# A Strassen pair whose sixth product has a PSUM bank of its own and whose seventh is issued behind the next pair's first, with PSUM tags by role and a later root and scan

## The chip, the cores and the metric

The kernel runs on one core of a Trainium2 chip. The metric is the device time of one execution in microseconds (us). The core's engines are TensorE (PE in the profile; PEld is its loading of stationary operands), VectorE (DVE), ScalarE (ACT), GpSimd (POOL) and SyncE (SP), which here only issues DMAs. Each engine works through its own queue of instructions in order. PE writes its sums to banks of PSUM, and DVE and ACT read them from there.

## The reference

The kernel computes one decoder block for one sequence of 2048 positions with a model width of 1024, in float32. Cut to what matters:

```python
h = rms_norm(x, g_norm) * (1 + scale) + shift        # shift, scale, gate from silu(c) @ w_mod
proj = h @ w_in                                       # 1024 -> 8 x 1024
x_rnn, z_rnn, q, k, v, z_attn, g_r, g_a = split(proj)
xc = causal_depthwise_conv(x_rnn)                     # width 4
r, i = sigmoid(xc @ w_a + b_a), sigmoid(xc @ w_x + b_x)   # 8 blocks of 128
a = exp(-8 * r * softplus(-lam)); bx = sqrt(1 - a * a) * i * xc
hr = scan(h_t = a_t * h_{t-1} + bx_t)                 # along the sequence
y_rnn  = (hr * silu(z_rnn)) @ w_out_rnn
o      = three dilated window attentions of rope(q), rope(k), v, merged
y_attn = (o * silu(z_attn)) @ w_out_attn
merged = sigmoid(g_r + b) * y_rnn + sigmoid(g_a + b) * y_attn
out = rms_norm(x + gate * (merged @ w_o), g_final)
```

## The kernel before

**Precision.** A float32 product is made of three matmuls: each operand is split into a high and a low part, and `mm3` (L150) sums high by high, high by low and low by high in one PSUM bank (the matmuls are recorded in `mm`, L148). An operand's high part is made by ACT (L202, L156), the low part by POOL (L162) or DVE (L165).

**The projection by Strassen pairs.** Every part of the projection but v is computed by Strassen and Winograd's scheme of seven products instead of eight. One pair covers two blocks of 128 output columns by two chunks of 512 positions (`CH`), that is one half of the sequence. There are 28 pairs, and the outer loop (L933 and on) goes through all of them twice, for the first half of the sequence (f = 0) and for the second (f = 1). A product sums four blocks of 128 along the contraction, so it is 4 x 3 = 12 matmuls of 128 x 512. The left operands are sums of blocks of the weights: for f = 0 they are formed as they are needed (`left_operands`, L250: the sums on DVE at L256, L257, L259 and L264, the split on ACT and POOL) in a ring of seven tiles S, and stored to DRAM (`sD`, from ACT's queue); for f = 1 they are loaded again from `sD` by SP's queue (`load_next`), each load following the product that frees a tile. The right operands, B11 to B22 and T1 to T4, are made once for each half.

`strassen` (L314) records the products of a pair in this order, with four PSUM tiles of the pool `pj`, which has five banks that rotate under one tag:

| product | right operand | bank | what reads the bank |
|---|---|---|---|
| 1 | B11 | X | ACT copies it to u1 (L340) |
| 2 | T2 | Z | DVE: u2 = Z + u1 (L341) |
| 3 | T3 | W | DVE: u3 = W + u2 (L346) |
| 4 | T1 | V | DVE: V + u3 is output block (1, 1), "ev4" |
| 5 | B21 | X, on top | ACT: X is output block (0, 0) |
| 6 | T4 | W, on top | DVE: W + u2 is block (1, 0), "ev6" |
| 7 | B22 | V, on top | DVE: V + u2 is block (0, 1), "ev7" |

The three evictions on DVE are `total` (L387); their destination is named ev, zs, xr or t after the kind of pair. Products 5, 6 and 7 accumulate onto what is in the bank, so 6 cannot start before u3 has read W, and 7 not before ev4 has read V. The pairs follow one another without a break, and a new tile takes the bank that was allocated five tiles earlier.

**The recurrence.** In each half eight of the pairs, one for each block m of the recurrence, hold x_rnn in their row 0 and z_rnn in row 1 (`recurrent`). Each is followed by one or two pairs for gates or for the part of q and k that isn't rotated ("plain"); 22 pairs make up this stage. After them come two pairs with rotated columns (`rotated_pairs`) and four plain ones. The steps of the recurrence are recorded at fixed distances, counted in products, behind product 5 of the pair for the first chunk and 7 products later for the second (`steps_after`, L775 and on): tap 0 (ACT makes xc, L714), taps 1 (three multiply-adds on DVE, L720), split 2, gates 4 (6 matmuls each into the pool `pg` of three banks), sigmoids 5 (L733), decay 6 (POOL L737, DVE L738), exponentials 7 (ACT Tanh, Exp, Square, L743 to L745), root 8 (DVE L749, ACT Sqrt L750), scan 9 (DVE: t times gi at L754, the scan at L755), finish 10 (DVE: times the gate zs, L760), then halves and store. zs has two buffers, xc one.

**What sets the order.** The attention and output part has an order written out by hand. In the projection the kernel records operations in program order, and a scheduler at build time lays out each engine's queue from its own estimate of durations; evictions, u1, u2 and u3 are recorded with high priority. At run time an instruction of a queue waits in place until what it needs is done, and all that stands behind it waits too.

## Time and profile before

| | us |
|---|---|
| three runs | 2355.1, 2352.55, 2354.84 |
| median | 2354.84 |
| the profiled execution | 2357.67 |
| its span, first to last instruction | 2355.9 |
| PE busy | 2232.7 |
| DVE busy | 1322.5 |
| ACT busy | 1187.2 |
| POOL busy | 953.0 |

The mean granted clock of TensorE is 0.983 of full speed. By stages, in us from the span's start: opening and values of f = 0 to about 210 (the first pairs start at 152); recurrence, gate and plain pairs of f = 0 from 210 to 640; rotated and last plain pairs to 752; values of f = 1 to 873; recurrence, gate and plain pairs of f = 1 to 1350; rotated and last plain pairs to 1448; attention, outputs and the final norm to the end.

A row of the timeline gives the start (us), the duration (us), engine, line, operation, output<-inputs by the program's names, shapes and the number of instructions joined in the row; in square brackets stands how long the engine idled before it, and what ended that. A row of the waits gives the engine, what it worked on, what it waited for, and then the total in us, the number of times and the longest. Matmuls are pipelined, so the end of one overlaps the start of the next.

### The profile page before, as it was taken

The page shows a single profiled execution, that of the slowest core. Times are in us where ns is not written, and L with a number is a line of the kernel's source. Part 1 is how long each engine was busy: PE and PEld are TensorE (multiplying, and loading weights), DVE is VectorE, ACT ScalarE, POOL GpSimd, SP SyncE. Part 2 cuts the span into 40 slices and gives each one's busy share as a digit, 9 for nine tenths or more (in the row PEclk, how much of TensorE's full clock was granted, in tenths as well). Part 3 has the DMA queues.
Part 4 walks back from the last instruction along what each step waited for, and adds up shares of the span by engine and source line. Part 5 has one row for each costly group of instructions (what it writes and reads, how often), then busy time and mean ns, then how long its engine had stood idle before and what let it go on. Part 6 is the DMA issues. An engine that isn't in the chain of part 4 may idle for free.

```text
span 2355.9 us, 33999 instructions
## 1 busy us (share of the span) xinstructions
PE 2232.7 (95%) x11397; PEld 1878.1 (80%) x11397; DVE 1322.5 (56%) x2430; ACT 1187.2 (50%) x2358; POOL 953.0 (40%) x732
## 2 busy tenths in 40 slices
PE   6999999999989999999999998989999898989998
PEld 6997777777777897778888876878888797968887
DVE  6837666757586625344544461456666778645343
ACT  4636656666642635555544411565667787622111
POOL 1356656665556534333211120354455656422000
PEclk9999999999999999999999999999999999999999
DMA  7376877677779669999777778888898888799732
GB/s 257 102 226 221 275 262 262 235 267 249 244 251 282 189 200 323 322 308 326 239 235 233 247 226 267 263 251 278 266 293 274 242 242 249 223 336 304 252 122 97
DMA packets 420946, 585.44 MB, mean 249 GB/s; under 512 B 72518, under 2 KB 278562, under 8 KB 419748
## 3 DMA queue, kind: packets, MB, share of 16 engines
q1 hardware_dynamic: 382932, 463.53, 63.4%
q10 hardware_dynamic: 37648, 119.70, 13.4%
q8 instruction: 90, 1.47, 0.3%
q14 instruction: 84, 0.69, 0.1%
q0 software_dynamic: 192, 0.05, 0.0%
HBM read 367.14 MB, written 216.01 MB: 248 GB/s over the span
## 4 chain that ended last, share of the span: by engine, by line
PE 59%; DMA 12%; DVE 8%; ACT 5%; issue 4%; POOL 2%; SPq 1%; ACTq 1%; DVEq 0%; POOLq 0%
PE pj L148 41%; PE pq L148 7%; PE o L148 4%; PE sc L148 4%; DMA R<-in_w_in_dram 2%; PE pg L148 1%; PE pT L1163 1%; POOL S L162 1%; DMA vraw<-vN 1%; PE pT L1176 1%; ACT L744 1%; DMA S<-sD 1%; DMA gw<-in_w_mod_dram 1%; DMA meT<-fg 1%; DMA wD<-s 1%
## 5 line engine op out<-in xcount | busy, mean ns | idle before, releaser
L148 PE MATMUL pj<-T,S 128*128 128x512 f32 x4704 | 1119.6, 397 | 30.0 <-DVE ev L387 17.9
L148 PEld LDWEIGHTS pj<-T,S 128*128 128x128 f32 x4704 | 887.6, 189 | 249.8 <-DVE ev L387 24.5
L148 PE MATMUL pj<-yh,S 128*128 128x512 f32 x1024 | 374.5, 409 | 17.7 <-ACT yh L156 10.3
L162 POOL TENSOR_TENSOR S<-R,S 128x512 fp32r<-128x512 f32 x168 | 245.7, 1474 | 272.4 <-ACT S L202 99.6
L148 PEld LDWEIGHTS pj<-yh,S 128*128 128x128 f32 x1024 | 197.0, 192 | 55.6 <-ACT yh L156 11.1
L148 PE MATMUL pj<-yl,S 128*128 128x512 f32 x512 | 204.9, 401 | 1.6 <-POOL yl L162 0.6
L1079 ACT ACTIVATE pp<-pp,st 128x256 f32<-128x256 f32 (+3 forms) x256 | 133.9, 524 | 114.2 <-DVE st L1078 113.4
L148 PE MATMUL pj<-S,T 128*128 128x256 f32 x1152 | 158.4, 292 | 4.6 <-ACT S L156 1.4
L148 PEld LDWEIGHTS pj<-S,T 128*128 128x128 f32 x1152 | 147.8, 196 | 6.2 <-POOL S L162 1.8
L162 POOL TENSOR_TENSOR S<-s,S 128x512 fp32r<-128x512 f32 x84 | 113.9, 1358 | 73.4 <-ACT S L202 39.0
L165 DVE TENSOR_TENSOR ptl<-pT,pth 128x384 fp32r<-128x384 f32 (+1 forms) x160 | 97.8, 628 | 67.1 <-ACT pth L156 64.9
L1078 DVE CUSTOM_DVE_ANT_0 pp<-sc,msk 128x256 f32<-128x256 f32 (+3 forms) x256 | 105.0, 449 | 32.3 <-PE sc L148 29.5
L720 DVE SCALAR_TENSOR_TENSOR xc<-xr,par,xc 128x512 f32<-128x512 f32 x96 | 84.1, 876 | 68.6 <-ACT xc L714 67.9
L1143 ACT ACTIVATE pp<-pp,M 128x256 f32<-128x256 f32 (+3 forms) x256 | 118.0, 523 | 9.0 <-DVE M L1267 9.0
L148 PEld LDWEIGHTS pj<-yl,S 128*128 128x128 f32 x512 | 98.8, 193 | 18.8 <-DMA yl<-yaT 2.7
L162 POOL TENSOR_TENSOR kq<-kraw,kq 128x512 fp32r<-128x512 f32 (+1 forms) x64 | 100.1, 1574 | 31.8 <-ACT kq L156 31.6
L341 DVE TENSOR_TENSOR u<-pj,u 128x512 f32<-128x512 f32 x56 | 38.4, 686 | 131.4 <-PE pj L148 81.6
L162 POOL TENSOR_TENSOR vh<-vraw,vh 128x256 fp32r<-128x256 f32 (+1 forms) x64 | 66.6, 1041 | 111.8 <-ACT vh L156 94.3
L162 POOL TENSOR_TENSOR wh<-vraw,wh 128x640 fp32r<-128x640 f32 (+1 forms) x32 | 48.4, 1511 | 129.1 <-ACT wh L156 60.5
L148 PE MATMUL pq<-ol,mh 128*128 128x512 f32 x256 | 100.5, 393 | 0.0
L148 PE MATMUL pq<-oh,mh 128*128 128x512 f32 x256 | 97.9, 393 | 2.1 <-ACT mh L156 2.1
L148 PE MATMUL pq<-oh,ml 128*128 128x512 f32 x256 | 99.5, 389 | 0.0
(297 smaller groups left out, 3848.0 us busy)
## 6 DMA issues: line engine op xcount, KB each, us to landing
sD<-S ACTq DMA_DIRECT2D x196, 512.0 KB, 3.9
S<-sD SPq DMA_DIRECT2D x196, 512.0 KB, 5.4
S<-wD SPq DMA_DIRECT2D x128, 512.0 KB, 5.6
R<-in_w_in_dram SPq DMA_DIRECT2D x136, 256.0 KB, 4.2
wD<-s ACTq DMA_DIRECT2D x64, 256.0 KB, 5.4
T<-in_w_mod_dram SPq DMA_DIRECT2D x8, 1024.0 KB, 11.6
vN<-ev SPq DMA_DIRECT2D x64, 128.0 KB, 2.1
zaT<-ev SPq DMA_DIRECT2D x32, 256.0 KB, 4.7
```

The source lines that it names most:

```text
L148: last_mm[0] = nc.tensor.matmul(o, lhsT=l, rhs=r, start=st, stop=sp, **kw).ins
L162: nc.gpsimd.tensor_tensor(o, i, h.bitcast(F32), ALU.subtract)
L165: return nc.vector.tensor_tensor(o, i, h.bitcast(F32), ALU.subtract).ins
L341: nc.vector.tensor_tensor(u2[:], Z[:], u1[:], ALU.add)
L720: nc.vector.scalar_tensor_tensor(xc, xr[:, i : i + CH], cw(i), xc, ALU.mult, ALU.add)
L744: nc.scalar.activation(a, y, AF.Exp, scale=-1.0)
L1078: nc.vector.tensor_tensor_reduce(pdst, s_ps, mask, 1.0, 3e38, ALU.add, ALU.min, m_)
L1079: nc.scalar.activation(pdst, pdst, AF.Exp, bias=m_, scale=-1.0, accum_out=l_)
L1143: nc.scalar.activation(pp, pp, AF.Copy, scale=w)
L1163: nc.tensor.transpose(pt[:, c0 + j * P : c0 + (j + 1) * P], pp[i][:, k * P : (k + 1) * P], ident)
L1176: nc.tensor.transpose(pt[:, c * P : (c + 1) * P], pp[:, half * P : (half + 1) * P], ident)
```

## The change

Five things are changed.

- Product 6 has a PSUM tile of its own, Y, of the tag "Z"; it no longer accumulates onto W, and output block (1, 0) is Y + u3 instead of W + u2. The bank W is finished with product 3.
- Product 7 isn't recorded at the end of its pair. It is kept in `behind` with its left operand already taken, and recorded by `last_product` after product 1 of the next pair (or at the end of a stage).
- The PSUM tiles of the pairs have tags by role: X with two banks, Z, W and V with one each, five in all as before. The value stage goes through them in the order X, Z, W, X, V (`pj_tile`).
- Root, scan and finish are recorded at 9, 11 and 12 products behind product 5 instead of 8, 9 and 10; halves and store follow at 12, for f = 1 at 13 and 14. zs has three buffers instead of two, and xc two instead of one.
- The loads of f = 1 follow the set of operands used, in order, since product 7's operand is now used after a later one. The tables of closures bind their loop variables, `finish_late` runs a step's list itself, and six of the seven `next_even` steps come one product later.

```diff
--- before.py
+++ after.py
@@ -213,7 +213,8 @@
 
     def finish_late():
         while late:
-            run_late(min(late))
+            for fn in late.pop(min(late)):
+                fn()
 
     def steps_after(start, steps):
         for lag, fn in steps:
@@ -279,7 +280,7 @@
 
 
 
-    loaded, n_loaded = [], [0]
+    loaded, n_loaded, used = [], [0], set()
 
     def load_next():
         n = n_loaded[0]
@@ -287,7 +288,7 @@
         if n < 28 * 7:
             t = s_tile([P, 2, KH, P])
             nc.sync.dma_start(t[:].bitcast(F32), sD[n])
-            loaded.append(t)
+            loaded.append((n, t))
         else:
             k = n - 28 * 7
             if k < 3:
@@ -319,40 +320,66 @@
             for _ in range(NS):
                 load_next()
 
-        def prod(ps, b, first, last):
-            s = loaded.pop(0) if f else next(ops)
+        def take():
+            return (f, *loaded.pop(0)) if f else (f, 7 * x, next(ops))
+
+        def prod(ps, b, first, last, op=None):
+            f, i, s = op or take()
             bh, bl = B[b]
             for k in range(KH):
                 mm3(ps[:], s[:, 0, k, :], s[:, 1, k, :], bh[:, k, :], bl[:, k, :],
                     first=first and k == 0, last=last and k == KH - 1, skip_group_check=True)
             n_prod[0] += 1
             if f:
-                load_next()
+                used.add(i)
+                while n_loaded[0] - NS in used:
+                    load_next()
             run_late(n_prod[0])
 
-        X = T(pj, [P, CH], F32, "pj")
+        X = T(pj, [P, CH], F32, "X", bufs=2)
         prod(X, "B11", True, False)
-        Z = T(pj, [P, CH], F32, "pj")
+        last_product()
+        Z = T(pj, [P, CH], F32, "Z")
         prod(Z, "T2", True, True)
         u1 = T(up, [P, CH], F32, "u1", bufs=1)
         u2 = T(up, [P, CH], F32, "u2", bufs=2)
         with tc.high_priority():
             nc.scalar.activation(u1[:], X[:], AF.Copy)
             nc.vector.tensor_tensor(u2[:], Z[:], u1[:], ALU.add)
-        W = T(pj, [P, CH], F32, "pj")
-        prod(W, "T3", True, False)
+        W = T(pj, [P, CH], F32, "W")
+        prod(W, "T3", True, True)
         u3 = T(up, [P, CH], F32, "u3", bufs=1)
         with tc.high_priority():
             nc.vector.tensor_tensor(u3[:], W[:], u2[:], ALU.add)
-        V = T(pj, [P, CH], F32, "pj")
+        V = T(pj, [P, CH], F32, "V")
         prod(V, "T1", True, False)
         done(1, 1, V, u3)
         prod(X, "B21", False, True)
         done(0, 0, X, None)
-        prod(W, "T4", False, True)
-        done(1, 0, W, u2)
-        prod(V, "B22", False, True)
-        done(0, 1, V, u2)
+        Y = T(pj, [P, CH], F32, "Z")
+        prod(Y, "T4", True, True)
+        done(1, 0, Y, u3)
+        op = take()
+
+        def last():
+            prod(V, "B22", False, True, op)
+            done(0, 1, V, u2)
+        behind.append(last)
+
+
+    behind = []
+
+    def last_product():
+        while behind:
+            behind.pop()()
+
+
+    pj_tags, n_pj = ("X", "Z", "W", "X", "V"), [0]
+
+    def pj_tile(shape):
+        tag = pj_tags[n_pj[0] % 5]
+        n_pj[0] += 1
+        return T(pj, shape, F32, tag, bufs=1 + (tag == "X"))
 
     def output_weights():
 
@@ -423,7 +450,7 @@
     pR = pools.open("pR", side="right", bufs=1)
     wS = pools.open("wS", side="right", bufs=1)
     wq = pools.open("wq", side="right", bufs=1)
-    pj = pools.open("pj", bufs=5, space=PSUM)
+    pj = pools.open("pj", bufs=1, space=PSUM)
     pg = pools.open("pg", bufs=3, space=PSUM)
     vx = pools.open("vx", bufs=1)
 
@@ -609,7 +636,7 @@
     def values_by_halves(ev, m, ws, n):
 
         names = ("B12", "B22") if n % 2 else ("B11", "B21")
-        pss = [T(pj, [P, 2, 256], F32, "pj") for g in range(2)]
+        pss = [pj_tile([P, 2, 256]) for g in range(2)]
         for kh in range(2):
             (hh, hl), (wh, wl) = B[names[kh]], ws[kh]
             for g in range(2):
@@ -634,7 +661,7 @@
 
         names = ("B12", "B22") if n % 2 else ("B11", "B21")
         for g in range(2):
-            ps = T(pj, [P, 2, 256], F32, "pj")
+            ps = pj_tile([P, 2, 256])
             for r in range(2):
                 js = slice((2 * g + r) * P, (2 * g + r + 1) * P)
                 for k in range(KT):
@@ -687,7 +714,7 @@
         start = [0]
 
         def z_part(j, ps, u):
-            z = zs[j] = T(rp, [P, CH], F32, "zs", bufs=2)
+            z = zs[j] = T(rp, [P, CH], F32, "zs", bufs=3)
             total(z[:], ps, u)
             sg = []
 
@@ -711,7 +738,7 @@
             def tap():
                 nc.scalar.activation(xr[:, 0:3], xtail[:, m, :], AF.Copy)
                 nc.scalar.activation(xtail[:, m, :], xr[:, CH : CH + 3], AF.Copy)
-                nc.scalar.activation(new("xc"), xr[:, 0:CH], AF.Identity, scale=cw(0),
+                nc.scalar.activation(new("xc", bufs=2), xr[:, 0:CH], AF.Identity, scale=cw(0),
                                      bias=par[:, C_CB + m : C_CB + m + 1])
 
             def taps():
@@ -774,7 +801,7 @@
                 start[0] = n_prod[0]
             steps_after(start[0] + 7 * j, (
                 (0, tap), (1, taps), (2, split), (4, gates), (5, sigmoids), (6, decay), (7, exponentials),
-                (8, root), (9, scan), (10, finish), (11 if f else 10, halves), (12 if f else 10, store)))
+                (9, root), (11, scan), (12, finish), (12 + f, halves), (12 + 2 * f, store)))
 
         def done(i, j, ps, u):
             (z_part if i else x_part)(j, ps, u)
@@ -842,7 +869,7 @@
     def rotated_pairs(qp, f, Ct, St):
 
         for base, dstT, qs in QK:
-            def rotated(i, j, ps, u):
+            def rotated(i, j, ps, u, dstT=dstT, qs=qs):
                 n = 2 * f + j
                 cq = slice(j * CH, (j + 1) * CH)
                 t0 = T(qp, [P, CH], F32, "t0", bufs=NT0[f])
@@ -873,7 +900,7 @@
             cuts.append(pieces)
         for base, dstT, qs in QK:
             for t in range(0, 6, 2):
-                def plain(i, j, ps, u):
+                def plain(i, j, ps, u, t=t, dstT=dstT, qs=qs):
                     n = 2 * f + j
                     t0 = plain_at[0]()
                     scaled(t0, ps, u, qs)
@@ -888,7 +915,7 @@
     def gate_pairs(ep, f):
         for m in range(0, KT, 2):
             for base, dst, b0 in ((5 * D, zaT, None), (6 * D, grT, C_BG), (7 * D, gaT, C_BG + 8)):
-                def gate(i, j, ps, u):
+                def gate(i, j, ps, u, m=m, dst=dst, b0=b0):
                     n = 2 * f + j
                     t = T(ep, [P, CH], F32, "ev", bufs=3)
                     v = ps
@@ -952,6 +979,7 @@
             for _ in range(1 + (m % 4 > 0)):
                 next(plain if n % 6 == 3 else gates)
                 n += 1
+        last_product()
         finish_late()
         pools.close("rp")
         qp = pools.open("qp", bufs=1)
@@ -971,7 +999,8 @@
             if n == 5 and f == 0:
 
                 for p in range(7):
-                    late.setdefault(n_prod[0] + p + 1, []).append(lambda p=p: next_even(p))
+                    late.setdefault(n_prod[0] + p + 1 + (p > 0), []).append(lambda p=p: next_even(p))
+        last_product()
         finish_late()
         for n in sorted(after_prod):
             run_late(n)
```

## The prediction, made before the changed kernel was run

> **What bounds the kernel now.** I read the head of the page first, then busy time by stage, then TensorE's waits, then the rows of single pairs.
>
> ```profile
> span 2355.9 us, 33999 instructions
> PE 2232.7 (95%) x11397; PEld 1878.1 (80%) x11397; DVE 1322.5 (56%) x2430; ACT 1187.2 (50%) x2358; POOL 953.0 (40%) x732
> ```
>
> TensorE (PE) is busy in 95% of the span; no other engine passes 56%. The change removes no matmul, so it can only win idle time of PE. The next view gives the busy time by stage (first column the window, second its length, then PE, PEld, DVE, ACT, POOL, the granted clock):
>
> ```profile
> 210.00:640.00 430.00, 407.27 (x1716) 322.78 (x1715) 276.55 (x301) 264.27 (x434) 258.25 (x184) 0.99 0.74 252
> 640.00:752.00 112.00, 103.94 (x451) 82.74 (x450) 80.68 (x136) 40.02 (x72) 59.68 (x41) 0.98 0.81 257
> 873.00:1350.00 477.00, 469.82 (x2012) 378.06 (x2011) 207.39 (x266) 243.92 (x383) 132.20 (x101) 1.00 0.85 280
> 1448.00:2356.00 908.00, 857.72 (x4770) 739.03 (x4768) 517.72 (x1301) 460.58 (x1163) 341.96 (x288) 0.97 0.79 245
> 1100.00:1200.00 100.00, 100.00 (x431) 80.63 (x430) 48.42 (x60) 54.85 (x88) 23.86 (x19) 1.00 0.77 251
> ```
>
> The recurrence and gate pairs run in 210 to 640 (first half of the sequence, f = 0) and 873 to 1350 (f = 1): PE idles 430.00 − 407.27 = 22.7 us in the first, 7.2 in the second. Attention and outputs (1448 to the end) are untouched by the edit, and in the two programs' orders by engine they are the same; I cost them at nothing. The last row gives the yardstick: 100.00 us held 431 matmuls without a gap, 0.232 us each, so a product of 12 takes 2.78 us, and two take 5.57. Who ends PE's idle time (total us, times, longest):
>
> ```profile
> PE pj L148 <- DVE ev L387: 17.9, 14, 3.3
> PE pj L148 <- DVE zs L387: 3.1, 2, 1.8
> PE pj L148 <- DVE u L346: 3.0, 2, 1.7
> PE pj L148 <- DMA S<-sD: 2.1, 1, 2.1
> ```
>
> The first three are the change's target. Their places, for two pairs of f = 0 (6, from 286 us, and 7), the longest (980.75), and one with a long tail (550.91):
>
> ```profile
> 298.81 5.96 PE L148 MATMUL pj<-T,S 128*128 128x512 f32 x25
> 305.41 8.20 PE L148 MATMUL pj<-T,S 128*128 128x512 f32 x34 [0.65 <-DVE ev L387]
> ...
> 325.11 3.05 PE L148 MATMUL pj<-T,S 128*128 128x512 f32 x12 [1.71 <-DVE u L346]
> 330.49 6.79 PE L148 MATMUL pj<-T,S 128*128 128x512 f32 x28 [2.33 <-DVE ev L387]
> ...
> 550.91 5.30 PE L148 MATMUL pj<-T,S 128*128 128x512 f32 x15 [2.22 <-DVE ev L387]
> ...
> 980.75 4.61 PE L148 MATMUL pj<-T,S 128*128 128x512 f32 x12 [3.31 <-DVE ev L387]
> ```
>
> 325.11 is product 6 of pair 7, which accumulates onto product 3's bank and waits until u3 (L346) has read it. 305.41, 330.49, 550.91 and 980.75 start product 7, which accumulates onto product 4's bank and waits for that product's eviction, ev4 (L387 on DVE). Why ev4 is late shows DVE's own queue:
>
> ```profile
> 302.92 1.23 DVE L720 SCALAR_TENSOR_TENSOR xc<-xr,par,xc 128x512 f32<-128x512 f32 x1 [3.26 <-ACT xc L714]
> ...
> 305.28 1.16 DVE L720 SCALAR_TENSOR_TENSOR xc<-xr,par,xc 128x512 f32<-128x512 f32 x1
> ...
> 307.57 1.80 DVE L720 SCALAR_TENSOR_TENSOR xc<-xr,par,xc 128x512 f32<-128x512 f32 x1
> 309.29 1.27 DVE L755 TENSOR_TENSOR_SCAN y<-a,htail,t 128x512 f32<-128x512 f32 x1
> 310.48 1.72 DVE L259 TENSOR_TENSOR R<-R,R 128x512 f32<-128x512 f32 x1
> 312.12 2.09 DVE L760 TENSOR_TENSOR zs<-y,zs 128x512 f32<-128x512 f32 x1
> 314.14 1.27 DVE L387 TENSOR_TENSOR ev<-pj,u 128x512 f32<-128x512 f32 x2
> ...
> 326.61 0.69 DVE L749 SCALAR_TENSOR_TENSOR t<-y,t 128x512 f32<-128x512 f32 x1 [1.55 <-ACT y L745]
> 329.14 0.69 DVE L754 TENSOR_TENSOR t<-t,gi 128x512 f32<-128x512 f32 x1 [1.84 <-ACT t L750]
> 329.75 0.68 DVE L387 TENSOR_TENSOR ev<-pj,u 128x512 f32<-128x512 f32 x1
> ...
> 335.46 0.69 DVE L259 TENSOR_TENSOR R<-R,R 128x512 f32<-128x512 f32 x1
> ...
> 336.66 0.69 DVE L387 TENSOR_TENSOR ev<-pj,u 128x512 f32<-128x512 f32 x1
> ```
>
> In pair 7, ev4 (329.75) stands behind L754 (t·gi), which waits 1.84 us for ACT's square root, and behind the root's L749, which waits 1.55. In pair 6 a convolution tap (L720) waits 3.26 us for ACT's xc in front of it.
>
> **The change part by part.**
>
> *What goes.* Product 6 gets a bank of its own, so the 3.0 us for u3 go. Product 7 comes a product (2.78) later, root and scan one and two products later, and in the changed program's order on DVE ev4 now stands ahead of t·gi: of the 17.9 + 3.1 us only what exceeds 2.78 could stay (3.31 − 2.78 = 0.5, and ev4 is earlier too). I take all: 24.0 us. Two of these waits have a tail at half clock: the 12 matmuls of 980.75 took 4.61 us where those of 325.11 took 3.05, and the 15 of 550.91 took 5.30 against 15 × 0.232 + 0.17 = 3.65; 1.6 each, 3.2 together. Together 27.2 us; the lower bound is nothing, if every wait reappears elsewhere. By the Trainium skill ("TensorE: Matmul & The Clock Gate", table of clock states) the half rate comes after an idle window of about 3.4 us; here 2.22 us of idle time were followed by it and 2.33 (330.49, 28 matmuls in 6.79) were not, so the trace departs from the page; by the rule neither tail would be due to its wait, and the sum would be 3.2 less.
>
> *What comes: product 2 of the next pair.* Product 6 of a pair and product 2 of the next now share the one bank "Z", so the next pair's second product must wait for ev6, product 6's eviction. Between lie the next product 1 and the late product 7: ev6 has 5.57 us from product 6's end. How late is it by the trace of before? Pair 6: the run from 298.81 holds the last 11 matmuls of product 5, the 12 of product 6, and 2 of the next product 1, so product 6 ended at 298.81 + 23 × 0.232 = 304.15; ev6 is the first of the two at 314.14 and ended at 314.82. That is 10.67, 5.1 over. Pair 7: product 6 (325.11) ended at 327.99, ev6 (336.66) at 337.35: 9.36, 3.8 over. The first and the last of the late pairs:
>
> ```profile
> 185.71 12.47 PE L148 MATMUL pj<-T,S 128*128 128x512 f32 x53
> 198.30 0.68 DVE L387 TENSOR_TENSOR ev<-pj,u 128x512 f32<-128x512 f32 x1
> ...
> 607.79 6.44 PE L148 MATMUL pj<-T,S 128*128 128x512 f32 x27
> 621.46 0.68 DVE L387 TENSOR_TENSOR ev<-pj,u 128x512 f32<-128x512 f32 x1
> ```
>
> Pair 1 (product 6 ends 18 matmuls into that run, 189.9; 9.1, 3.5 over) and pair 20 (25 matmuls in, 613.6; 8.5, 3.0 over). Of pairs 1 to 20, fifteen are over, by 46.5 us together. That is the upper end for f = 0. Two things shorten it. In the changed order the three taps of the second xc no longer stand between ev4 and ev6 but ahead of u2, five products earlier: without the time they take there (pair 6: 3.97 us of the rows 302.92, 305.28 and 307.57; 2.5 to 2.9 in the other such pairs) 20.8 us are left. And the waits of L749 and L754 (3.4 us in pair 7), inside the same stretch in seven pairs, shrink with the later root and scan, whose inputs from ACT are then a product or two old; those seven (2, 4, 7, 10, 13, 15, 18: 11.9 of the 20.8) then come to about nothing. What stays are pairs 1, 3, 6, 9, 12, 17 and 20: 0.8, 0.9, 1.1, 1.6, 1.7, 2.7, 0.1: 8.9 us. For f = 1, DVE is emptier (207 us busy in 477), and only pair 30 is far over, by 8.6, of which 3.5 are this:
>
> ```profile
> 946.00 0.69 DVE L387 TENSOR_TENSOR zs<-pj,u 128x512 f32<-128x512 f32 x1 [3.49 <-DMA yaT<-zs]
> ```
>
> With three zs buffers that wait goes, taps take 2.3; I keep 2.9. New waits: 11.8 us, bounds 0 and 46.5. I take a value near the low end because the instructions that make the lateness are seen to move.
>
> The Trainium skill speaks against me here ("SBUF — State Buffer", Who interferes with whom): a VectorE instruction with two SBUF inputs and a GpSimd one that reads SBUF block each other for a whole instruction. The rows agree: L259 takes 1.72 us at 310.48 and 0.69 at 335.46. Were one more such meeting to fall ahead of ev6 in each of the seven pairs, 7 × 1.03 = 7.2 us would be added.
>
> *Next product 4 behind ev7.* One bank "V": the next product 4 waits for product 7's eviction, which has two products again, products 2 and 3. ev7 follows ev6 directly (314.14, x2), and product 7 is itself a product later; I take 0, bounds 0 and 2.8 (one product).
>
> *Later root and scan, one xc buffer more.* The same instructions, later. The last recurrent pair of each half runs out over more products, all covered by PE's. The changed program has one table load more:
>
> ```profile
> L750 ACT ACT_TABLE_LOAD x32 | 41.1, 1283 | 1.6 <-DMA S<-sD 1.0
> ```
>
> 1.28 us on ACT, busy 264 of 430: 0, at most 1.3.
>
> *Product 7's operand held longer.* One of seven S tiles comes free a product later, in f = 1 also its reload on SP's queue. The only wait for a reload is the 2.1 us above; 0, bounds −2.1 and +2.8.
>
> *Rotated pairs, 640 to 752.* Evictions there wait for the rotary tables:
>
> ```profile
> 687.65 0.69 DVE L387 TENSOR_TENSOR t<-pj,u 128x512 f32<-128x512 f32 x1
> ```
>
> This is ev7 of pair 22, 25 us after its product. In the changed order pair 23's product 4 must follow it; the order puts three other products (pair 24's 1, 3 and 5) ahead of it. Counting products to the start of that product 4, 15 precede in both. I take 0, ±3. In the opening the value tiles rotate through the banks by role: ±2.
>
> Sum: −24.0 − 3.2 + 11.8 = −15.4 us. The profiled execution took 2357.67 (span 2355.9), 2.8 over the median 2354.84; against the first 2342.3, against the second 2339.4. **Predicted: 2339 us.**
>
> **The rivals.**
>
> *A. Everything goes.* No new wait: 2354.8 − 27.2 = 2328. For it: the changed order and the emptier f = 1 half. Against it: ev6 still follows scan, finish, s1 and R on DVE, 4 to 7 us of work.
>
> *B. The gap moves.* The waits of L749 and L754 stay although recorded later, because ACT is equally late; then new waits are 20.8 + 2.9 = 23.7 and the time is 2354.8 − 27.2 + 23.7 = 2351. For it: the planner had already put the next product 1 ahead of product 7 in places (the 2 matmuls at the end of 298.81's run), so this edit is partly there.
>
> *C. The Z bank binds (slower).* One mechanism: product 2 of the next pair waits for ev6, with DVE's queue as long as before because the taps, moved ahead of u2, still push everything behind them back by their 3.26 us wait for ACT. The lateness is then the 46.5 us, and the time 2354.8 − 27.2 + 46.5 = 2374. It decides from 27.2 / 15 = 1.8 us per late pair on, that is from ev6 7.4 us after product 6. Against it: five products lie between u2 and ev6, and DVE is idle 36% of that stage.
>
> **How the numbers follow.** My forecast (2332 to 2346) has 0.45, A 0.17, B 0.18, C 0.20. What a measurement can tell from no change is 0.2%, 4.7 us: faster is under 2350.1, slower over 2359.5. Faster: 0.45 + 0.17 + a third of B = 0.68; same: the rest of B, 0.12; slower: C, 0.20. The range reaches below to A with 3 us of the rotated pairs (2325) and above into the milder half of C (2361), which leaves about 0.05 and 0.13 out.
>
> **What would show it.** Right: the waits of PE for ev at product 7 and for u at product 6 gone, new ones at product 2 of the next pair of 5 to 20 us together, all in f = 0 and at most 2.7 each, PE idle under 14 us in the stage that is now 210 to 640; no zs wait for a DMA on DVE; the attention stage still 908 us. Wrong: waits at product 2 or 4 of over 27 us; an L720 or L754 that waits for ACT still in front of ev4 or ev6; half-clock windows after new gaps of over 2.2 us; or a rotated stage longer than 115 us.

## The result

The changed kernel takes 2359.8 us (median) beside 2354.26 us for the kernel before: 1.0023 times as long, 95% interval 1.0012 to 1.0034. Forecast were 2339 us and a range that ended at 2361 with the chances on faster; it went the other way, by 5.5 us.

The profiled execution of the changed kernel took 2354.95 us (span 2353.2), at the low end of its runs. Its page still says that TensorE is busy in 95% of the span. The stages tell more, bounded here and below by the first matmul of pairs 0, 22, 28 and 50 in each trace (columns as before: window, length, PE, PEld, DVE, ACT, POOL, granted clock, DMA share, GB/s). First the kernel before, pairs 0 to 21 of f = 0 and of f = 1:

```profile
152.27:640.63 488.36, 462.77 (x1946) 367.19 (x1945) 320.14 (x343) 297.94 (x491) 298.28 (x211) 0.99 0.75 254
...
873.82:1336.45 462.63, 455.45 (x1946) 366.34 (x1945) 203.33 (x255) 242.59 (x381) 132.20 (x101) 1.00 0.85 279
```

Then the changed kernel, the same pairs:

```profile
146.21:645.75 499.54, 466.48 (x1947) 372.81 (x1945) 342.74 (x345) 299.88 (x493) 301.26 (x213) 0.97 0.72 250
...
880.14:1334.86 454.72, 453.59 (x1947) 365.21 (x1945) 205.28 (x255) 244.15 (x381) 131.57 (x101) 1.00 0.85 285
```

The f = 1 pairs gained 7.9 us, and hold almost no idle time (454.72 − 453.59 = 1.1 us). The f = 0 pairs lost 11.2 us, with VectorE 22.6 us longer busy, and TensorE's clock granted at 0.97 instead of 0.99. The rest of the span in these two executions: opening 152.3 to 146.2, rotated pairs and values 233.2 to 234.4, rotated pairs of f = 1 126.8 to 123.0, attention and outputs 892.6 to 895.3. Over all the traces of this study the opening lies between 144.7 and 152.3 us and the attention part between 887.6 and 898.0, also among kernels whose orders there are the same, so these two are scatter and hide 5.5 us easily in one execution; the medians of the runs decide. What TensorE waits for in the changed kernel:

```profile
PE Z L148 <- DVE ev L414: 32.4, 11, 6.2
...
PE X L148 <- ACT t L863: 4.8, 1, 4.8
...
PE Z L148 <- DVE t L414: 3.8, 2, 2.3
```

The waits of products 6 and 7 of the kernel before (24.0 us) are gone, every one. In their place stands product 2 of the next pair, which waits for ev6 on the shared bank Z: 32.4 us, all but 0.3 of it in the f = 0 pairs. Two of these on TensorE, at pair 10 (waiting for ev6 of pair 9) and at pair 15 (for ev6 of pair 14):

```profile
368.87 2.96 PE L148 MATMUL X<-T,S 128*128 128x512 f32 x12
371.66 2.95 PE L148 MATMUL V<-T,S 128*128 128x512 f32 x12
376.31 1.87 PE L148 MATMUL Z<-T,S 128*128 128x512 f32 x7 [1.70 <-DVE ev L414]
...
491.99 5.43 PE L148 MATMUL Z<-T,S 128*128 128x512 f32 x12 [6.17 <-DVE ev L414]
```

The product behind the wait of 6.17 us took 5.43 us where 2.95 is usual: the granted clock was 0.50 from 494 to 497. VectorE in front of the first of them, where pair 9's product 6 ended at 368.9:

```profile
369.23 0.69 DVE L781 TENSOR_TENSOR t<-t,gi 128x512 f32<-128x512 f32 x1 [0.17 <-ACT t L777]
369.96 2.20 DVE L782 TENSOR_TENSOR_SCAN y<-a,htail,t 128x512 f32<-128x512 f32 x1
372.19 1.08 DVE L787 TENSOR_TENSOR zs<-y,zs 128x512 f32<-128x512 f32 x1
373.19 0.68 DVE L257 TENSOR_TENSOR s<-R,R 128x512 f32<-128x512 f32 x1
373.90 1.66 DVE L260 TENSOR_TENSOR R<-R,R 128x512 f32<-128x512 f32 x1
375.49 0.68 DVE L414 TENSOR_TENSOR ev<-Z,u 128x512 f32<-128x512 f32 x1
```

and GpSimd beside it:

```profile
369.73 1.34 POOL L162 TENSOR_TENSOR S<-s,S 128x512 fp32r<-128x512 f32 x1 [1.81 <-ACT S L202]
373.56 3.13 POOL L162 TENSOR_TENSOR S<-R,S 128x512 fp32r<-128x512 f32 x2 [2.49 <-ACT S L202]
```

There is hardly a wait in this stretch. VectorE works without pause and ev6 comes last: t·gi, scan, finish, the two operand sums, then ev6, 7.0 us where 5.57 are free. The scan takes 2.20 us and L260 1.66 while GpSimd splits an operand at the same time. Taken over the ten late pairs (1, 3, 6, 7, 9, 12, 14, 17, 18, 20), product 6's end to ev6's end adds up to 89.8 us, 76.3 of it VectorE at work, 8.7 waiting for ACT and 4.1 for a weight load. The longest of the ten waits, the 6.17 us above, is of the other kind: in pair 14 VectorE waited for ACT, at the root and at t·gi:

```profile
481.47 0.69 DVE L776 SCALAR_TENSOR_TENSOR t<-y,t 128x512 f32<-128x512 f32 x1 [1.90 <-ACT y L772]
486.05 0.69 DVE L781 TENSOR_TENSOR t<-t,gi 128x512 f32<-128x512 f32 x1 [3.88 <-ACT t L777]
```

### The profile page after: what moved, and what is told of

Read it like the earlier page. It is cut to its first block, busy times and chain, and to the rows that moved or that the text cites. A ratio compares the mean times of both kernels' runs of the same rounds, so it can differ in the third digit from the quotient of the medians.

```text
span 2353.2 us, 33986 instructions
## 1 busy us (share of the span) xinstructions
PE 2229.5 (95%) x11397; PEld 1878.9 (80%) x11397; DVE 1336.7 (57%) x2430; ACT 1191.6 (51%) x2359; POOL 953.6 (41%) x732
## 4 chain that ended last, share of the span: by engine, by line
PE 54%; DMA 8%; DVE 3%; ACT 2%; issue 1%; POOL 1%; SPq 0%; ACTq 0%; POOLq 0%; DVEq 0%
PE pj L148 12%; PE pq L148 7%; PE Z L148 7%; PE V L148 6%; PE X L148 6%; PE o L148 4%; PE sc L148 4%; PE W L148 3%; DMA wD<-s 2%; PE pT L1192 1%; PE pT L1205 1%; PE pg L148 1%; DMA vraw<-vN 1%; DMA meT<-fg 1%; DMA R<-in_w_out_rnn_dram 1%
## 5 line engine op out<-in xcount | busy, mean ns | idle before, releaser
L148 PE MATMUL Z<-T,S 128*128 128x512 f32 x1344 | 342.9, 405 | 36.6 <-DVE ev L414 32.4
L148 PEld LDWEIGHTS Z<-T,S 128*128 128x128 f32 x1344 | 258.7, 194 | 103.9 <-issue 25.7
L148 PE MATMUL X<-T,S 128*128 128x512 f32 x1344 | 334.3, 397 | 4.8 <-ACT t L863 4.8
L148 PE MATMUL V<-T,S 128*128 128x512 f32 x1344 | 331.9, 395 | 1.8 <-DMA S<-sD 1.0
L148 PEld LDWEIGHTS X<-T,S 128*128 128x128 f32 x1344 | 253.9, 189 | 64.9 <-ACT t L863 5.0
L148 PEld LDWEIGHTS V<-T,S 128*128 128x128 f32 x1344 | 252.5, 188 | 62.0 <-DVE t L414 2.6
L148 PE MATMUL W<-T,S 128*128 128x512 f32 x672 | 170.6, 395 | 0.0
L148 PEld LDWEIGHTS W<-T,S 128*128 128x128 f32 x672 | 126.4, 188 | 30.7 <-issue 0.9
L747 DVE SCALAR_TENSOR_TENSOR xc<-xr,par,xc 128x512 f32<-128x512 f32 x96 | 94.9, 989 | 59.3 <-ACT xc L741 58.4
L1107 DVE CUSTOM_DVE_ANT_0 pp<-sc,msk 128x256 f32<-128x256 f32 (+3 forms) x256 | 105.3, 449 | 37.5 <-PE sc L148 34.7
```

What stands on the lines that cost most here:

```text
L148: last_mm[0] = nc.tensor.matmul(o, lhsT=l, rhs=r, start=st, stop=sp, **kw).ins
L747: nc.vector.scalar_tensor_tensor(xc, xr[:, i : i + CH], cw(i), xc, ALU.mult, ALU.add)
L1107: nc.vector.tensor_tensor_reduce(pdst, s_ps, mask, 1.0, 3e38, ALU.add, ALU.min, m_)
```

## The experiments

Stage lengths in us of each profiled execution, and the ratio to the kernel before with its interval. A stage length is that of one execution. Kernels that have the same order of instructions in a stage show how far it scatters: in f = 0 the changed order took 499.5, 500.9, 501.1 and 502.2 (changed, e6, e7, e3) and the old one under five tags 491.5, 492.4, 493.3 and 493.6 (e13, e5, e16, e10); in f = 1 the old order took 460.8 to 464.3 in five executions, but one other order 453.9 and 461.4 (e8, e10). The ratio is that of the medians of several executions.

| kernel | ratio (95%) | f = 0 pairs | f = 1 pairs |
|---|---|---|---|
| before | 1 | 488.4 | 462.6 |
| changed | 1.0023 (1.0012–1.0034) | 499.5 | 454.7 |
| e1_two_z | 1.0021 (1.0005–1.0037) | 494.2 | 457.9 |
| e2_six_on_w | 0.9981 (0.9966–0.9997) | 493.8 | 455.0 |
| e3_old_lags | 1.0002 (0.9990–1.0014) | 502.2 | 457.0 |
| e4_seven_in_place | 1.0017 (1.0001–1.0034) | 502.1 | 455.4 |
| e5_second_half_only | 0.9930 (0.9909–0.9951) | 492.4 | 458.2 |
| e6_first_half_only | 1.0035 (1.0018–1.0053) | 500.9 | 463.9 |
| e7_scan_13 | 1.0016 (1.0000–1.0033) | 501.1 | 456.0 |
| e8_buffers_only | 0.9962 (0.9941–0.9983) | 496.6 | 453.9 |
| e9_old_buffers_f0 | 1.0035 (1.0020–1.0050) | 503.8 | 456.2 |
| e10_buffers_f1 | 0.9949 (0.9932–0.9966) | 493.6 | 461.4 |
| e11_banks_only | 1.0030 (1.0009–1.0051) | 502.3 | 454.1 |
| e12_late_f0 | 1.0043 (1.0025–1.0061) | 505.9 | 459.6 |
| e13_five_tags | 0.9959 (0.9942–0.9976) | 491.5 | 464.3 |
| e14_roles_f0 | 0.9991 (0.9972–1.0010) | 490.1 | 462.9 |
| e15_late_rotating_f0 | 1.0044 (1.0022–1.0067) | 507.1 | 460.8 |
| e16_banks_f1 | 0.9924 (0.9903–0.9945) | 493.3 | 455.6 |
| e17_short_scan | 0.9936 (0.9911–0.9961) | 480.9 | 454.1 |
| e18_pool_writes | 0.9837 (0.9810–0.9863) | 464.0 | 456.5 |

### One part undone at a time

Two banks for Z (in the value stage too):

```diff
-        Z = T(pj, [P, CH], F32, "Z")
+        Z = T(pj, [P, CH], F32, "Z", bufs=2)      # product 6's tile Y likewise
-    pg = pools.open("pg", bufs=3, space=PSUM)
+    pg = pools.open("pg", bufs=2, space=PSUM)
```

> Edit: the tag Z gets two PSUM banks, taken from the pool of the gate matmuls (3 to 2); all else as in the changed kernel. Theory Z (the one bank shared by product 6 and the next pair's product 2 is what costs the time: 32.4 us of waits for ev there): these waits fall under 5 us, the stage of the f = 0 pairs falls from 499.5 us to about 465 to 475, the time to about 2325 to 2335. Theory L (the later root and scan put the scan in front of both evictions on DVE, whatever bank): the waits move to product 4 (V behind ev7), over 15 us there, the time stays above 2350. Cost of the third gate bank: at most the gate rows' waits, under 5 us.

The waits at Z went, and nothing was won; 1.0021. The f = 0 pairs came down by 5.3 us, to 494.2, but the rotated pairs and values rose from 234.4 to 243.0. In the f = 0 pairs TensorE now waited for this (waits, in that stage):

```profile
PE pg L148 <- ACT xh L156: 12.7, 6, 5.3
PE V L148 <- ACT t L777: 4.6, 3, 3.7
PE V L148 <- ACT S L202: 3.4, 1, 3.4
PE V L148 <- DVE ev L414: 2.5, 1, 2.5
PE pg L148 <- POOL xl L162: 2.1, 4, 0.5
```

Theory Z as I put it falls: the bank is where VectorE's lateness is felt, not its source. Theory L's stand-in, product 4, is not where it went either. That the same lateness now reaches TensorE by xh, which comes from the taps on VectorE, is an argument and wasn't tested. (One gate bank fewer may have a share in it; that wasn't separated.)

Product 6 on W:

```diff
-        Y = T(pj, [P, CH], F32, "Z")
-        prod(Y, "T4", True, True)
-        done(1, 0, Y, u3)
+        prod(W, "T4", False, True)
+        done(1, 0, W, u2)
```

> Edit: product 6 accumulates on W again (evicted with u2), seventh product late, tags and lags as in the changed kernel. Product 2 of the next pair then waits for nothing of this pair, and ev6 has three products (8.4 us) until the next product 3. By the changed kernel's profile ev6 is over 8.4 us late in six pairs of f = 0, 11.5 us together, and u3 is over 5.57 us late in four, 4.4 us together. Theory Z: the waits in f = 0 fall from 32 to about 16 us, the time to about 2343. Theory L: the scan still stands in front of ev6, waits of 25 us or more at product 3, the time stays at 2355 to 2360.

0.9981, and f = 0 at 493.8: between the two expectations. The waits in that stage were 14.8 us for u3 at product 6, in 16 places, and 8.3 for ev6 (ev and zs) at product 3.

The old lags:

```diff
-                (9, root), (11, scan), (12, finish), (12 + f, halves), (12 + 2 * f, store)))
+                (8, root), (9, scan), (10, finish), (11 if f else 10, halves), (12 if f else 10, store)))
```

> Edit: root, scan, finish, halves and store at their old distances (8, 9, 10), all else as in the changed kernel. Theory L: without the later scan ev6 comes earlier, waits for ev at Z fall from 32.4 to about 10 us, the time to about 2338. Theory Z: the scan at distance 9 lies in front of ev6 as well, the waits at Z stay at 25 us or more, and t times gi waiting for the root is back in front of ev4 and ev6; the time is 2358 to 2370.

The planner lays out the same order of instructions on every engine with the old lags as with the new ones. So this kernel is the changed kernel a second time: the 32.4 us of waits for ev at Z became 36.4 (32.7 of them in f = 0), the f = 0 pairs 502.2. Its ratio of 1.0002 beside 1.0023 (and 1.0016 for e7, which has that order too) shows that ratios from different sets of runs agree to 0.2% and no better. Theory L falls: the later root, scan and finish of the change do nothing.

Product 7 in its place:

```diff
-        behind.append(last)
+        last()
```

> Edit: product 7 is recorded in its own pair again, behind product 6; product 6 keeps its own bank, tags and lags as in the changed kernel. Product 2 of the next pair still comes two products after product 6. Theory Z: the waits at Z stay at 25 us or more, and some at product 7 for ev4 come back (up to 10 us); the time is 2358 to 2372. If the late seventh product is itself what costs (it pushes ev7, and with it the next product 4): the time falls to that of the kernel before, 2354, or under it.

Nearly as theory Z expected: 24.3 us of waits for ev at Z and 12.4 at product 7; 1.0017.

### By halves

For these and the next the banks come from five tags of one bank each; for a half "by role" X alternates between two of them and Z, W, V keep one, for a half that "rotates" a new tile takes the next one in turn:

```diff
+    def bank(role, f, shape=(P, CH)):
+        if ROLE[f]:
+            n_x[0] += role == "X"
+            k = {"X": 3 * (n_x[0] % 2), "Z": 1, "W": 2, "V": 4}[role]
+        else:
+            k = n_pj[0] % 5
+            n_pj[0] += 1
+        return T(pj, list(shape), F32, f"b{k}")
```

Own bank for product 6 (`OWN6`), late product 7 (`LATE7`), roles (`ROLE`), zs and xc buffers, and lags are then set for each half; of two values the first is for f = 0.

```diff
+OWN6, LATE7, ROLE = (False, True), (False, True), (False, True)
+ZS, XC = (2, 3), (1, 2)
```

> Edit: all of the change for f = 1 alone; f = 0 has product 6 on W, product 7 in place, the old lags and buffers, and banks that rotate (under five tags of one bank each). By the profiles the changed kernel took 11.2 us more for the f = 0 pairs and 7.9 + 3.8 us less for the f = 1 pairs and rotated pairs. Theory H (the halves are independent; the change loses in f = 0 where DVE also makes the operands, and gains in f = 1): f = 0 pairs back at 488 us, f = 1 pairs at 455, the time 10 to 12 us under the kernel before, about 2343 to 2348. Rival N (the stages' differences are one execution's scatter): the time is that of the kernel before within 4 us.

0.9930, a median of 2340.3 us beside 2358.1: theory H, though 17.8 us are more than the 10 to 12 that it gives (see e13 for the rest). The f = 0 pairs took 492.4, the f = 1 pairs 458.2.

```diff
+OWN6, LATE7, ROLE = (True, False), (True, False), (True, False)
+ZS, XC = (3, 2), (2, 1)
```

> Edit: all of the change for f = 0 alone, f = 1 as before. Theory H: f = 0 pairs at 500 us, f = 1 pairs at 462 to 463, the time 11 us or more over the kernel before, about 2368. Rival N: within 4 us of the changed kernel, 2358 to 2362.

1.0035, 2368.0 beside 2358.1, with f = 0 at 500.9 and f = 1 at 463.9: theory H again.

### Order and buffers

```diff
+LAGS = ((11, 13, 14, 14, 14), (9, 11, 12, 13, 14))    # root, scan, finish, halves, store
```

> Edit: the changed kernel with the root of f = 0 at distance 11, scan 13, finish, halves and store 14, so that the scan and finish are recorded two products further from product 6. Theory Q (the waits of product 2 in f = 0 come from scan, finish and operand sums that stand in front of ev6 in DVE's queue): waits for ev at Z fall from 32 to under 15 us, f = 0 pairs from 500 to 485 to 490. Rival E (whatever is moved away, the stage's time is set by the chain of DVE, ACT and POOL for operands and recurrence, and another wait takes its place, as with two banks for Z): f = 0 pairs stay at 492 to 502.

Here too the planner's order on TensorE, VectorE and GpSimd is that of the changed kernel; 35.2 us of waits at Z, f = 0 at 501.1. Theory Q wasn't tested by it, since the scan did not move. A third execution of the same order, it shows that the loss in f = 0 is no scatter: 499.5, 502.2, 501.1 and, with e6, 500.9. Against the old design under five tags (491.5 to 493.6) it is 6 to 11 us.

```diff
+OWN6, LATE7, ROLE = (False, False), (False, False), (False, False)
+ZS, XC = (3, 3), (2, 2)
```

> Edit: the kernel before with zs in three buffers and xc in two, nothing else of the change (its five rotating banks under five tags). If the moved taps and the freed zs are what gains in f = 1: f = 1 pairs near 458, and the time 4 to 6 us under the kernel before. If taps ahead of u2 are what slows DVE in f = 0 (there 357 us busy against 338): DVE's busy time of the f = 0 pairs rises to 350 or more and that stage is longer than 488. If the buffers do nothing without the rest: all stages as before.

0.9962, the same as the control e13 below (0.9959), so the buffers alone win nothing in all. In f = 0 they cost 3 to 5 us against the order of that control (496.6 and 491.5 to 493.6), and VectorE's durations there sum to 351 us (338 before, 357 changed): the second expectation. In f = 1 the pairs took 453.9.

```diff
+OWN6, LATE7, ROLE = (True, True), (True, True), (True, True)
+ZS, XC = (2, 3), (1, 2)
```

> Edit: the changed kernel with one xc and two zs buffers in f = 0, as before (f = 1 keeps two and three). Theory X (in f = 0 the second xc buffer is what costs: the taps run earlier, beside POOL's splits, and leave DVE waiting at the root with ev4 and ev6 behind it; 8 of the 11 us, as the kernel with the buffers alone showed): DVE's busy time of the f = 0 pairs back at 338 to 343 us, that stage at 488 to 492, the time about 2345 to 2350. Theory Z (the shared bank of products 6 and 2 costs by itself): waits for ev at product 2 stay over 20 us and the stage at 497 or more, the time at 2356 or more.

503.8 in f = 0 with VectorE's durations still 351 us in sum: theory X falls, the buffers aren't needed for the loss. The waits for ev and zs in that stage were 19.0 us, a little under what theory Z had set, with 10.6 us for xh beside them.

```diff
+OWN6, LATE7, ROLE = (False, False), (False, False), (False, False)
+ZS, XC = (2, 3), (1, 2)
```

> Edit: the kernel before, with three zs and two xc buffers for f = 1 alone; no other part of the change. If the f = 1 gain of the change is the buffers' (the changes to products 6 and 7 and the banks add nothing): f = 1 pairs at 453 to 456 us, the time within 3 us of the kernel with all of the change in f = 1, 2340 to 2344, 0.993 of the kernel before. If the banks have a part in it: 4 us or more over that.

0.9949, most of which the control shows as well. The f = 1 pairs took 461.4 here and 453.9 in e8, although the two kernels have the same order of instructions in them on every engine; so 7.5 us lie between two executions, and these lengths don't decide. The medians do: neither e8 nor e10 is clear of the control.

```diff
+OWN6, LATE7, ROLE = (True, True), (True, True), (True, True)
+ZS, XC = (2, 2), (1, 1)
```

> Edit: products 6 and 7 and the banks by role as in the changed kernel, old lags and old buffers in both halves. Theory Z: f = 0 pairs at 497 us or more, with over 20 us of waits for ev at product 2. Theory X: f = 0 pairs at 488 to 492. In f = 1 the pairs take 462 us if the buffers make the gain there, 455 if the banks do.

502.3 and 454.1, with 23.0 us of waits for ev and zs in f = 0: products 6 and 7 and the roles make both the loss in f = 0 and the gain in f = 1.

```diff
+OWN6, LATE7, ROLE = (False, True), (True, True), (True, True)
+ZS, XC = (2, 3), (1, 2)
```

> Edit: f = 0 with product 6 on W and old buffers but product 7 late and banks by role; f = 1 with all of the change but the lags. ev4 has a product more and product 2 waits for nothing of the pair before; product 6 waits for u3 and the next product 3 for ev6, 8.4 us after product 6. If that is the better half of the change in f = 0: f = 0 pairs at 478 to 486, the time about 2335. If another wait takes the place of each that goes: 490 to 494, and the time about that of the change in f = 1 alone, 2340 to 2345.

505.9 in f = 0, worse than either expectation: 12.1 us of waits in that stage for u3 at product 6, and 13.1 for ev6 (ev and zs). (The profiled execution took 13.7 us more than the median, 2363.9; that too is far over both expectations.) Its f = 0 pairs differ from those of e2 only by the old buffers and lags, and e2 took 493.8 there and 0.9981 in all: so what a late product 7 costs depends on the buffers. Larger numbers of them help here and cost in e8; why is open.

### Which part of the banks

```diff
+OWN6, LATE7, ROLE = (False, False), (False, False), (False, False)
+ZS, XC = (2, 2), (1, 1)
```

> Edit: the kernel before with its five rotating banks under five tags of one bank each, taken in turn; nothing of the change. If the tags are only names: within 3 us of the kernel before, f = 0 pairs 488 to 494, f = 1 pairs 461 to 464. If naming the banks is what gained in the kernels with the change in f = 1 alone or the buffers alone: 8 to 14 us under the kernel before.

0.9959, 2348.5 beside 2358.4: the tags aren't only names. The planner lays out another order with them (by the traces, 200 of TensorE's 11397 instructions and 140 of VectorE's 2430 stand at another place), with 5 us less in the rotated pairs and values (228.1) and 3 us less in the opening, the latter within the scatter; the f = 0 and f = 1 pairs of this execution took 3.1 and 1.7 us more. So of the 18 us that e5 is under the kernel before, about 10 are this and about 8 the change in f = 1.

```diff
+OWN6, LATE7, ROLE = (False, False), (False, False), (True, False)
```

> Edit: banks by role for f = 0 (X two, Z, W and V one each), products 6 and 7 where and as they were, old buffers and lags. Between product 6 and the next tile on its bank W lie then three products (8.4 us) where the rotation gave four. Theory S (the slack of the rotation is what f = 0 lives on): waits at product 3 for ev6 appear, f = 0 pairs at 496 us or more. Rival P (roles alone are harmless; product 6's own bank or the late product 7 costs): f = 0 pairs at 488 to 494, as the control.

490.1 in f = 0: theory S falls for the pairs, fixed roles alone cost nothing there. They cost in the rotated pairs (237.3 against 228.1), with the wait of 4.8 us for X that the changed kernel has too.

```diff
+OWN6, LATE7, ROLE = (False, False), (True, False), (False, False)
```

> Edit: product 7 late in f = 0 with the five rotating banks, product 6 on W, old buffers and lags. Theory S: ev4 has a product more (waits at product 7, about 20 us with what follows them, shrink to under 8) and the rotation leaves ev6 three to four products, so f = 0 pairs fall to 478 to 486. Rival P with the late product as the cost: f = 0 pairs at 496 us or more.

507.1 in f = 0, with all five banks rotating: rival P. Its waits in that stage are for a gate's eviction on VectorE (L946), xh and u3:

```profile
PE b L151 <- DVE ev L946: 12.9, 4, 3.8
PE pg L151 <- ACT xh L159: 10.1, 2, 8.2
PE b L151 <- DVE u L356: 9.7, 8, 2.9
```

The waits at product 7 are gone and more time is lost in other places: 37.5 us of waits in all, where the control has 29.4.

```diff
+OWN6, LATE7, ROLE = (False, True), (False, True), (False, True)
+ZS, XC = (2, 2), (1, 1)
```

> Edit: for f = 1 alone product 6 in its own bank, product 7 late, banks by role, with old lags and old buffers (one xc, two zs). If the banks make the gain of f = 1: f = 1 pairs at 453 to 456, the time within 3 us of the kernel with all of the change in f = 1 (2340). If the buffers make it: f = 1 pairs at 460 or more, the time within 4 us of the control.

0.9924, a median of 2342.2 beside 2358.4, f = 1 at 455.6 where the control has 464.3: the banks, with product 6's own bank and the late product 7, make the gain of f = 1. The slowest of its executions (2344.5) is faster than the fastest of the control (2345.5). This and e5 beat both kernels.

### VectorE's work, shortened

Scan and finish of f = 0 on a quarter of their columns; the rest of the recurrence's output of the first half is left out.

```diff
-                nc.vector.tensor_tensor_scan(y, v["a"][:], t, htail[:, m : m + 1], ALU.mult, ALU.add)
+                w = slice(0, CH if f else 128)
+                nc.vector.tensor_tensor_scan(y[:, w], v["a"][:, w], t[:, w], htail[:, m : m + 1], ALU.mult, ALU.add)
+                w = slice(0, 128 if f else 32)      # in finish, on both operands
```

> Edit: the changed kernel with scan and finish of f = 0 on a quarter of their columns (the rest of the recurrence's output of the first half is left out). PE's order is the same but for 8 of 11333 matmuls. Theory W (VectorE's work in front of ev6 is what product 2 waits for): scan from 2.2 to about 0.6 us and finish from 1.3 to 0.4, 2.4 us less in front of each ev6; waits for ev at product 2 fall from 32 to about 12 us, f = 0 pairs from 500 to 478 to 486, the time to about 2340. Rival E (another wait takes its place): the f = 0 pairs stay above 492.

The f = 0 pairs of this kernel, and its waits there:

```profile
149.52:630.45 480.93, 460.19 (x1946) 367.67 (x1945) 303.59 (x342) 297.94 (x490) 292.56 (x211) 0.99 0.75 258
```

```profile
PE Z L148 <- DVE ev L414: 18.4, 8, 6.2
PE Z L148 <- DVE zs L414: 1.6, 2, 1.1
```

480.9: 18.6 us less than the changed kernel, theory W, although the waits at Z fell to 20.0 us and not to 12, and the quarter scan still took 1.35 us on average and not 0.6. VectorE 39 us less busy brought half of that on TensorE; 27 of the 39 are scan and finish themselves, 9 are L260 (23.1 us instead of 31.9).

GpSimd writes zeros for the low parts of the weights in f = 0 and reads nothing for it; the low-order correction of these operands is left out in both halves.

```diff
-        lo_pool(t[:, 1], src, t[:, 0])
+        nc.gpsimd.memset(t[:, 1].bitcast(F32), 0.0)
```

> Edit: the changed kernel with the low parts of the weight operands of f = 0 written as zeros by GpSimd instead of subtracted (the low-order correction of the weights is left out for both halves, since f = 1 loads them again); the planner lays out another order for it. If GpSimd's reads are what lengthens VectorE's instructions: scan, root and operand difference at 1.3, 0.7 and 0.7 us, VectorE's busy time of the f = 0 pairs from 357 to 300 or less, f = 0 pairs at 480 or less. If the lengthening has another cause: VectorE busy 340 us or more. If the blocking is there but not what PE waits for: VectorE at 300, the stage above 492.

Its f = 0 pairs, and TensorE's waits in them:

```profile
149.24:613.27 464.03, 454.65 (x1946) 364.74 (x1945) 258.57 (x344) 300.38 (x491) 155.96 (x211) 1.00 0.79 268
```

```profile
PE Z L148 <- DVE ev L414: 4.5, 4, 1.5
PE V L148 <- DVE ev L414: 2.2, 1, 2.2
PE Z L148 <- DVE zs L414: 2.2, 1, 2.2
```

The scan and the operand difference as groups of this stage (busy us, then the mean in ns), in the kernel before,

```profile
L259 DVE TENSOR_TENSOR R<-R,R 128x512 f32<-128x512 f32 x22 | 27.8, 1262 | 0.4
L755 DVE TENSOR_TENSOR_SCAN y<-a,htail,t 128x512 f32<-128x512 f32 x16 | 25.3, 1584 | 0.0
```

in the changed kernel,

```profile
L782 DVE TENSOR_TENSOR_SCAN y<-a,htail,t 128x512 f32<-128x512 f32 x16 | 34.4, 2148 | 0.5
L260 DVE TENSOR_TENSOR R<-R,R 128x512 f32<-128x512 f32 x23 | 31.9, 1386 | 0.4
```

and with GpSimd only writing:

```profile
L782 DVE TENSOR_TENSOR_SCAN y<-a,htail,t 128x512 f32<-128x512 f32 x16 | 20.5, 1279 | 0.1
L260 DVE TENSOR_TENSOR R<-R,R 128x512 f32<-128x512 f32 x23 | 15.7, 684 | 0.4
```

The blocking is there and it is large: VectorE falls from 342.7 us busy to 258.6, and the stage from 499.5 to 464.0, with 9.4 us of idle time on TensorE. Part of the 35 us may be GpSimd's own shorter time (301 to 156 us) and the other order that the planner laid out; what is measured cleanly are VectorE's durations. Within this one trace ten of the 16 scans run beside GpSimd's writing alone, and they take 1.27 or 1.28 us like the others.

## Why the prediction was wrong

- *What goes* (24.0 us and two tails) was right: no wait at product 6 or 7 for u, ev or zs is left in the pairs. In f = 1, where nothing took their place, the stage fell by 7.9 us in the profile, where 5.0 + 1.3 of waits and a tail of 1.6 had been counted; that the two agree to the tenth is luck, since other executions with this order of f = 1 took 456.0 to 459.6 us instead of 454.7.
- *What comes: product 2 of the next pair* was the step that failed. The place and the limit of 5.57 us were right, the pairs too (1, 3, 6, 9, 12, 17 and 20 are among the ten), the size wrong: 32.1 us in f = 0 instead of 8.9, with longer half-clock tails behind them (0.97 for 0.99 over the stage). I took the lateness of ev6 in the old trace and subtracted what would move out of the stretch. The queue didn't empty: scan, finish and the operand sums stayed or moved in front of ev6, 7.6 us of work on average where 5.57 fit. The prediction named this work itself ("4 to 7 us"), under rival A, and didn't set it against the 5.57. Pairs 7, 14 and 18, counted at nothing, came with 10.8 of the 32.1 us; in pair 14 the waits of root and t·gi for ACT, which the later root and scan were to remove, are most of it.
- The weighed rule of the Trainium skill ("SBUF — State Buffer", Who interferes with whom) was the right one, and 7.2 us too little for it. In pair 9 the scan at 2.20 and L260 at 1.66 instead of 1.28 and 0.68 (e18) are 1.9 us; ev6 ended 7.3 us after product 6, and would have ended at 5.4, in time. Estimated in this way for all ten late pairs, from the short times that the same instructions have elsewhere in the trace, pairs 6, 9, 17 and 18 would have been in time, and the lateness beyond 5.57 us would be about 15 us instead of 34; most of what is left is in pairs 1, 14 and 20, in the last of which VectorE waited 4.1 us for a weight load. The runs agree with the page's distinction: with GpSimd only writing beside them, VectorE's two-input instructions keep their short times (e18).
- *Later root and scan* was taken to shrink the waits of L749 and L754 to nothing. Recording them later does nothing at all: the planner's order is the same with three sets of distances (changed, e3, e7). The waits for ACT at the root rose from 9.6 to 22.5 us in the stage, those at t·gi fell from 14.9 to 7.4.
- The taps did move ahead of u2, as the orders showed, but run beside GpSimd more often there (34 of 48 instead of 24): they took 54.8 us instead of 44.8.
- *Rotated pairs* (0, ±3) measured +1.2 us, values included; the new wait for X of 4.8 us is paid for by others that went. The later products and table load cost nothing visible.
- Rival C had the place, the decision point (1.8 us per late pair; 3.2 came about) and the sign right, and blamed the wrong thing, the taps' wait for ACT, which fell from 25.6 to 11.2 us in the stage; its time, 2374, was too long because 32 us of waits came and not 46.5.
- The other weighed rule of the Trainium skill, on the clock ("TensorE: Matmul & The Clock Gate", table of clock states), bears on the tails: in the changed kernel a wait of 1.70 us (376.31) was followed by full speed, one of 6.17 by half. The traces tell why 2.22 us were followed by half speed and 2.33 not: the granted clock changes on a grid of 3.41 us, and the 2.22 us lie within one step of it (547.7 to 551.1), while the 2.33 are divided over two, 1.1 and 1.2. The prediction was right to keep the tails.

What stays open: which part of the change makes the loss in f = 0. Product 6's own bank with product 7 in place (e4) and a late product 7 without that bank (e12, e15) each lose as much as both together, roles alone lose nothing (e14), and the late product 7 with the new buffers (e2) hardly anything (493.8). So it is also open why a late product 7 with rotating banks (e15) loses 16 us against its control; VectorE's load is the common factor, but the way from there to each wait was only argued. Also open is the gain of 10 us from the five tags.

## What to carry to other kernels

A wait on a bank names the engine that is late, not its cause: count the work that stands in front of the eviction on that engine and set it against the time the new order leaves, since moving one wait away only uncovers the next while that engine's queue is full. Give such an edit to the stage where the evicting engine has room (f = 1 here: 0.992 to 0.993, of which the tags alone make 0.996), and leave the crowded one as it was. Before a step is moved by a recorded distance in a kernel whose order a scheduler lays out, compare the resulting order of instructions: here the distances changed nothing.

## What the runs showed of the hardware

GpSimd's reading made VectorE's scan 2.15 us on average instead of 1.28 and a sum of two SBUF operands 1.39 instead of 0.68 in this stage; taking the reads away freed 84 us of VectorE in 500. A scan over a quarter of the columns took 1.39 to 1.50 us in the 15 places where it met a GpSimd instruction, and 0.48 in the one where it met none (e17): the addition of about 0.92 us is that of the whole scan (2.20 instead of 1.28).

Which of the two started first decided in these rows. In the f = 0 pairs of the changed kernel 15 of the 16 scans began while a GpSimd instruction was under way and took 2.19 to 2.30 us; the one that met none took 1.28. The operand sum L257 took 0.98 to 1.79 us in the 8 places where GpSimd had started first, and 0.67 to 0.70 in the 10 where VectorE had. t·gi met GpSimd in 14 of 16 places, had always started first, and took 0.69 in all.

The granted clock of TensorE changes on a grid of 3.41 us. Between 150 and 1448 us in all 20 traces of this study, each step at full clock in which TensorE idled over 1.89 us was followed by a step at half clock, and none in which it idled under 1.51; in the kernel before the border lies between 1.74 and 1.79, in the changed one between 1.69 and 1.92. What counts is the idle time within one step, so a wait that is divided over two of them goes unpunished more easily.
